# Retention's sample queries as a column of ones against weighted states

## The chip, the cores and the metric

The kernel runs on one core of a Trainium2 chip, as one launch. The metric is the device time of that launch in microseconds (us). A core has TensorE (PE, matrix products into PSUM; its weight loads are listed apart as PEld), VectorE (DVE), ScalarE (ACT), GpSimd (POOL) and SyncE (SP), which here issues the DMAs. Each engine runs its own queue of instructions in order, and semaphores tie the queues together.

## The reference

The reference is one layer of a decoder trunk: a half-step feed-forward block, a mixer, and a second half-step feed-forward block, each followed by a layer norm. The mixer adds a retention branch (8 heads of 256) and an HGRN2 branch (16 heads of 128). There are 272 prompt tokens (16 of them learned meta tokens) and 8 sample tokens; each sample has its own recurrent state, which is read, updated, written out and queried. For a sample, the chunk has one token, so retention comes down to this:

```python
def retention_chunk(S, q, k, v):
    C = q.shape[2]
    lg = retention_log_decay()
    ...
    o = jnp.einsum('bhij,bhjv->bhiv', inner, v) + jnp.einsum('bhid,bhdv->bhiv', q_dec, S)
    ...
    S_new = jnp.exp(lg * C)[:, None, None].astype(S.dtype) * S + jnp.einsum('bhjd,bhjv->bhdv', k_dec, v)
    return S_new.astype(S.dtype), o
```

With one token the two terms of `o` together are the query times the new state: o[v] = sum over d of q[d] * S_new[d, v], with d and v from 0 to 255. That sum, for 8 samples and 8 heads, is what the change computes in another way. It is followed by the head's layer norm (subtract the mean over v, divide by the deviation).

## The kernel before

All activations are kept with the features on the 128 partitions and the 280 tokens (272 and 8) along the free dimension. All large weights are streamed from memory in units of eight 128x128 blocks (512 KB): SyncE loads `raw` (line 185), ScalarE rounds it to `whi` (line 188), VectorE takes the rest `wlo` (line 189), and TensorE multiplies three times for each block, `whi` by the high and low part of the activations and `wlo` by the high part (line 218). `raw`, `whi` and `wlo` have three buffers each.

TensorE's order is the order of the program. The instructions of all other engines are ordered by the compiler's scheduler by readiness and priority; the weight stream has high priority. In the mixer the projections run group by group, and small steps of the two branches are put between their matmuls by hand: `mix_hg` and `mix_ret` are generators, one for each head pair or head `u`, and after each step k of a projection `pump` is called once. A `yield n` in a generator means that it goes on n pump calls later. A pump call comes after the blocks of one k, so after six matmuls where the group has two outputs.

`mix_ret(u, ...)` for head `u`: the states of the 8 samples come in four tiles `sms[2 * e + c]` of tag `smr`, where `e` is the half of the samples (0 to 3, 4 to 7) and `c` the chunk of 128 of the 256 state rows d. A tile has 128 partitions (d) by 4 samples by 256 columns (v). ScalarE multiplies each tile with the decay (line 1192), VectorE adds key times value (line 1198, one instruction for each sample and chunk), and SyncE writes the tile to the output `srs` (line 1202). The tag `smr` has four buffers, which `ks` and `vs`, two operands of the prompt's state, use as well.

After some more pump calls come the sample queries into the PSUM bank `pq` (tile name `pqr`): the score product of the last 16 prompt tokens (`scores`, line 1141), and then, for each sample and chunk, a matmul with a 128x32 stationary operand cut from `qdr`, in which one column holds the sample's query and the others are zero. The output goes to the 32 PSUM partitions `32 * j`, so that four samples can be in four column groups of the array at a time; each group adds up two samples (e = 0 and 1), in row e of its 32, and two chunks. These are 16 matmuls of 256 columns for each head, and each of these float32 matmuls stands in the trace as two records. The helper `alone` copies the queries into `qdr` before that. Then ScalarE copies the bank to `os` (line 1217), VectorE centres it, and seven pump calls later the head's output `por` is built.

Of the kernel before, what the change touches and what calls it, by code (L numbers as in the profile page):

```python
# [13 lines left out]
AF = mybir.ActivationFunctionType  # L14
ALU = mybir.AluOpType
# [3 lines left out]
P = 128  # L19
# [4 lines left out]
NMETA, SEQ, NS = 16, 256, 8  # L24
# [27 lines left out]
ALONE = 4 * 32 + 1  # L52
# [76 lines left out]
def trunk(ctx: ExitStack, tc: tile.TileContext, A, O):  # L129
    nc = tc.nc  # L130
# [12 lines left out]
    def mx_bank(name):  # L143
        return ps_m.tile([P, 512], F32, tag="mx", name=name)
# [94 lines left out]
    def mul(out, a, b):  # L239
        nc.vector.tensor_tensor(out=out, in0=a, in1=b, op=ALU.mult)  # L240
# [306 lines left out]
    with tc.tile_pool(name="yp", bufs=1) as yp:  # L547
# [7 lines left out]
        with tc.tile_pool(name="mp", bufs=1) as mp:  # L555
# [7 lines left out]
            def tmp(name, shape=(P, T), bufs=1, dt=F32, tag=None):  # L563
                if name in rows:
                    rows[name] = rows[name][1:] + rows[name][:1]
                    return rp.tile(list(shape), dt, tag=rows[name][-1], name=name)
                return mp.tile(list(shape), dt, tag=tag or name, name=name, bufs=bufs)
# [19 lines left out]


            qdh = tmp("qdh", (P, 4, ALONE))
            qdr = tmp("qdr", (P, 4, ALONE))  # L590
            nc.gpsimd.memset(qdh, 0.0)
            nc.gpsimd.memset(qdr, 0.0)
            qdh_at = [qdh.rearrange("p a c -> p (a c)")[:, 256 * h :] for h in range(2)]
            qdr_at = [qdr.rearrange("p a c -> p (a c)")[:, 2 * ALONE * c :] for c in range(2)]
            vsm = tmp("vsm", (P, P))
            vt2 = tmp("vt2", (P, 2, P))
            scr2 = tmp("scr2", (P, NMETA))
# [50 lines left out]
            def evacuate(n, c0, c1, o0, o1, b0, b1):  # L648
# [33 lines left out]
                elif n == "v_r":  # L682
                    v = tmp("v", (P, 2, T))
                    nc.scalar.copy(v[:, 0, :], o0)
                    nc.scalar.copy(v[:, 1, :], o1)
                    start(mix_ret(c0 // 2, st["q_r"], st["k_r"], v), 24 if c0 == 2 else 3)
                elif n in ("g_r", "g_h"):
                    sg = tmp("gs", (P, TL), bufs=2)
                    t = tmp("gt", (P, TL), bufs=2)
                    nc.scalar.activation(sg, o0, AF.Sigmoid)  # L690
                    mul(t, sg, o0)
                    sa = tmp("gs", (P, TL), bufs=2)
                    nc.scalar.activation(sa, o1, AF.Sigmoid)
                    mul(t, t, sa)
                    u, e = divmod(c0, 2)
                    while u not in (done_r if n == "g_r" else done_h):
                        pump()
                    if n == "g_r":
                        y = tmp("y", (P, TL))
                        mul(y, t, on_r[u][:, e, :])  # L700
                        st["y"] = y
                    else:
                        y = st["y"]
                        nc.vector.scalar_tensor_tensor(
                            out=t, in0=t, scalar=ngt[:, c0 : c0 + 1], in1=on_h[u][:, e, :], op0=ALU.mult, op1=ALU.mult)

                        ys[c0] = y if c0 < EARLY else yp.tile([P, TL], F32, tag=f"y{c0}", name=f"y{c0}")
                        add(ys[c0], y, t)
                        if c0 < EARLY:
                            split(yh[c0], yl[c0], y)  # L710
# [22 lines left out]
            def alone(qd, q):  # L733
                nc.vector.tensor_copy(
                    qd[:, :, : 128 : 32].rearrange("p (c e) j -> p c e j", e=2),
                    q[:, :, SEQ:].rearrange("p c (e j) -> p c e j", e=2))
# [348 lines left out]
            def mix_ret(u, q, k, v):  # L1085
# [3 lines left out]
                calm = 2  # L1089
                sms = []  # L1090
# [13 lines left out]
                for c in range(2):  # L1104
# [22 lines left out]
                    for x, g, his, i, lo in todo:  # L1127
                        for hi in his:
                            nc.scalar.activation(hi, x, AF.Copy, scale=g)
                        nc.vector.scalar_tensor_tensor(  # L1130
                            out=lo, in0=x, scalar=g, in1=his[i].bitcast(F32), op0=ALU.mult, op1=ALU.subtract)
                    yield 2
                alone(qdr, q)
                vts = [vt[:, 0], vt[:, 1], vs2]
                vrow = rows_out(vt2.rearrange("p c f -> p (c f)")[16:24, :], 256, "vr")

# [25 lines left out]
                for c in range(2):  # L1162
# [9 lines left out]
                    if c == 0:  # L1172
                        gams = [tmp("gam", (P, 1))]
                        nc.gpsimd.tensor_scalar(
                            out=gams[0], in0=so[:, 0:1], scalar1=GAMMA[u], scalar2=GAMMA[u], op0=ALU.min, op1=ALU.max)
# [13 lines left out]
                for e in range(2):  # L1189
# [3 lines left out]
                    for i in (2 * e, 2 * e + 1):  # L1193
                        for c in range(2):
                            for b in (2 * i, 2 * i + 1):
# [3 lines left out]
                                    out=x, in0=vbs[i][:, b - 2 * i, :], scalar=kk, in1=x, op0=ALU.mult, op1=ALU.add)  # L1199
# [1 line left out]
                    for c in range(2):  # L1201
                        nc.sync.dma_start(O["srs"][u, c, :, 4 * e : 4 * e + 4, :], ss[c])
                    yield 1 if e else 10 if u == 0 else 6
                yield (11 if u == 0 else 15) + 2 * calm
                pq = mx_bank("pqr")
                scores(pq[:, 256:], 2)
                for e in range(2):
                    for c in range(2):
                        for j in range(4):
                            b = 4 * e + j  # L1210
                            nc.tensor.matmul(  # L1211
                                pq[32 * j : 32 * j + 32, :256], qdr_at[c][:, 32 * b : 32 * b + 32],
                                sms[2 * e + c][:, j, :], start=e + c == 0, stop=e + c == 2, tile_position=(0, 32 * j))
                mul(scr2[:NB2], pq[:NB2, 256 : 256 + NMETA], dt[:NB2, c2:])
                upper_upper_lower(sc2, scr2[:NB2])
                os = tmp("osr", (P, 256))
# [160 lines left out]
```

## Time and profile before

| | |
|---|---|
| Time, median of 3 runs | 2567.76 us (2565.30 to 2568.72) |
| Profiled execution, span from its first to its last instruction | 2563.9 us |
| Granted TensorE clock | 1.000 |
| TensorE busy | 2553.4 us |
| VectorE busy | 1702.8 us |
| ScalarE busy | 1392.2 us |
| Sample-query matmuls `pqr<-smr,qdr` | 256 records, first at 859.8 us, last at 1698.6 us |

The profile is one execution. Its span leaves out what lies ahead of the first and behind the last instruction; the runs' times are 1.4 to 4.8 us above it. Rows of the timeline give the start in us, how long the row's instructions took together, the engine, the line, the operation with output and inputs by name, and how many instructions there are; in brackets stands the idle time ahead of it and what ended it. SPq marks the DMA issues of SyncE. Rows of groups give the count, then busy us and mean ns of one, then idle us before them. Rows of a tile give minimum, median and maximum ns.

### The profile page before, as it was taken

Reading aid. Unit: us, or ns where it says so; the run is one execution under the profiler, and the core shown is the slowest. Engines: PE = TensorE matmul, PEld = TensorE weight load, DVE = VectorE, ACT = ScalarE, POOL = GpSimd, SP = SyncE. Lnnn points to the kernel's source line nnn. Section 1 sums busy time; section 2 is a strip of 40 time slices with the busy share of each in tenths; the row PEclk is TensorE's granted clock in tenths of the full one; section 3 lists DMA queues with packets and bytes.
Section 4 is the critical chain, followed back from the end, with each engine's and each line's share of the span. In section 5 each row is a group of like instructions: output and inputs, shape, how many; then the busy total and the mean of one; then the engine's idle time right before and its main releaser. Section 6 shows DMA issues by size and latency. Waiting matters only on the chain.

```text
span 2563.9 us, 56275 instructions
## 1 busy us (share of the span) xinstructions
PE 2553.4 (100%) x23424; PEld 2534.4 (99%) x23424; DVE 1702.8 (66%) x2827; ACT 1392.2 (54%) x2186; POOL 57.0 (2%) x152
## 2 busy tenths in 40 slices
PE   9999999999999999999999999999999999999999
PEld 9999999999999999999999999999999999999998
DVE  6444544475569878777777777777885555556555
ACT  5444444444456767767676666675564444444443
POOL 0000000000000000000000000000000000000000
PEclk9999999999999999999999999999999999999999
DMA  7555555555555876767676767675556565565554
GB/s 244 183 187 183 187 182 184 186 182 186 184 201 180 287 265 232 264 214 260 212 264 215 259 223 255 224 239 188 196 190 197 194 197 195 194 196 195 195 195 149
DMA packets 156897, 536.26 MB, mean 209 GB/s; under 512 B 17952, under 2 KB 25952, under 8 KB 156640
## 3 DMA queue, kind: packets, MB, share of 16 engines
q1 hardware_dynamic: 156352, 532.37, 62.0%
q8 instruction: 183, 3.00, 0.5%
q14 instruction: 74, 0.61, 0.1%
q10 hardware_dynamic: 288, 0.29, 0.0%
HBM read 501.99 MB, written 30.61 MB: 208 GB/s over the span
## 4 chain that ended last, share of the span: by engine, by line
PE 96%; DVE 2%; ACT 0%; issue 0%; DMA 0%; SPq 0%; ACTq 0%; DVEq 0%
PE up L218 36%; PE dn L218 19%; PE pj_i_h L218 3%; PE pj_g_r L218 3%; PE pj_q_h L218 3%; PE pj_g_h L218 3%; PE pj_a_r L218 3%; PE pj_a_h L218 3%; PE pj_f L218 3%; PE pj_q_r L218 3%; PE pj_k_r L218 3%; PE wo L218 3%; PE pj_v_r L218 3%; DVE wlo L189 1%; PE pqr L1211 1%; PE psr L1168 0%
## 5 line engine op out<-in xcount | busy, mean ns | idle before, releaser
L189 DVE TENSOR_TENSOR wlo<-raw,whi 128x1024 fp32r<-128x1024 f32 (+1 forms) x869 | 1062.2, 1223 | 740.7 <-ACT whi L188 737.3
L188 ACT CAST whi<-raw 128x1024 fp32r<-128x1024 f32 (+1 forms) x870 | 905.7, 1042 | 909.2 <-PE up L218 411.0
L218 PE MATMUL up<-xh,whi 128*128 128x280 f32 (+1 forms) x2624 | 725.6, 280 | 0.6 <-ACT whi L188 0.6
L218 PE MATMUL up<-xh,wlo 128*128 128x280 f32 (+1 forms) x2624 | 725.8, 280 | 0.4 <-DVE wlo L189 0.3
L218 PE MATMUL up<-xl,whi 128*128 128x280 f32 (+1 forms) x2624 | 725.4, 279 | 0.0
L218 PEld LDWEIGHTS up<-xh,wlo 128*128 128x128 f32 x2624 | 492.6, 189 | 1.0 <-DVE wlo L189 1.0
L218 PEld LDWEIGHTS up<-xh,whi 128*128 128x128 f32 x2624 | 492.6, 189 | 0.8 <-ACT whi L188 0.8
L218 PEld LDWEIGHTS up<-xl,whi 128*128 128x128 f32 x2624 | 492.6, 189 | 0.0
L218 PE MATMUL dn<-hh,whi 128*128 128x280 f32 (+1 forms) x1376 | 384.7, 280 | 0.0
L218 PE MATMUL dn<-hh,wlo 128*128 128x280 f32 (+1 forms) x1376 | 384.3, 279 | 0.0
L218 PE MATMUL dn<-hl,whi 128*128 128x280 f32 (+1 forms) x1376 | 384.3, 279 | 0.0
L218 PEld LDWEIGHTS dn<-hh,whi 128*128 128x128 f32 x1376 | 260.1, 189 | 0.1
L218 PEld LDWEIGHTS dn<-hl,whi 128*128 128x128 f32 x1376 | 260.1, 189 | 0.1
L218 PEld LDWEIGHTS dn<-hh,wlo 128*128 128x128 f32 x1376 | 260.1, 189 | 0.0
L218 PE MATMUL pj_k_r<-xh,whi 128*128 128x280 f32 x256 | 74.2, 290 | 0.0
L218 PE MATMUL pj_g_r<-xh,whi 128*128 128x264 f32 x256 | 74.0, 289 | 0.0
L218 PE MATMUL pj_v_r<-xh,whi 128*128 128x280 f32 x256 | 73.8, 288 | 0.0
L218 PE MATMUL pj_v_r<-xh,wlo 128*128 128x280 f32 x256 | 72.4, 283 | 0.3 <-DVE wlo L189 0.3
L218 PE MATMUL pj_g_h<-xh,whi 128*128 128x264 f32 x256 | 72.7, 284 | 0.0
L218 PE MATMUL pj_k_r<-xh,wlo 128*128 128x280 f32 x256 | 72.4, 283 | 0.0
L218 PE MATMUL pj_v_r<-xl,whi 128*128 128x280 f32 x256 | 72.3, 283 | 0.0
L218 PE MATMUL pj_k_r<-xl,whi 128*128 128x280 f32 x256 | 72.3, 283 | 0.0
(421 smaller groups left out, 5263.4 us busy)
## 6 DMA issues: line engine op xcount, KB each, us to landing
raw<-in_w_up SPq DMA_DIRECT2D x343, 512.0 KB, 4.1
raw<-in_w_in SPq DMA_DIRECT2D x320, 512.0 KB, 4.3
raw<-in_w_dn SPq DMA_DIRECT2D x172, 512.0 KB, 3.5
smr<-in_sr SPq DMA_DIRECT2D x32, 512.0 KB, 5.0
out_srs<-smr SPq DMA_DIRECT2D x32, 512.0 KB, 6.7
raw<-in_w_out SPq DMA_DIRECT2D x32, 512.0 KB, 3.9
vbr<-vrd SPq DMA_DIRECT2D x32, 256.0 KB, 4.1
smh<-in_sg SPq DMA_DIRECT2D x16, 512.0 KB, 5.2
```

The source lines that it names most:

```text
L188: nc.scalar.copy(hi[:, j:jn, :], raw[:, j:jn, :])
L189: nc.vector.tensor_tensor(out=lo[:, j0:j1, :], in0=raw[:, j0:j1, :], in1=hi[:, j0:j1, :].bitcast(F32), op=ALU.subtract)
L218: nc.tensor.matmul(o, w, t, start=start, stop=stop)
L1211: nc.tensor.matmul(pq[32 * j : 32 * j + 32, :256], qdr_at[c][:, 32 * b : 32 * b + 32], sms[2 * e + c][:, j, :], start=e + c == 0, stop=e + ...
```

## The change

ScalarE multiplies the new state's chunk 0 in place with the sample's query (a scale for each partition), and VectorE adds chunk 1 times its part of the query, into the same tile. TensorE then needs only the sum over the 128 partitions: a stationary operand `one` with a column of ones in column e takes the place of `qdr`, and there are 8 matmuls for each head in place of 16. The weighting of e = 0 is placed 10 pump calls (head 0) or 14 (other heads) after the last state's update, that of e = 1 five later, and the matmuls five after that; before, the matmuls came after 15 or 19. `alone` is no longer called for retention.

```diff
             qdh = tmp("qdh", (P, 4, ALONE))
-            qdr = tmp("qdr", (P, 4, ALONE))
+            one = tmp("one", (P, 2, 32))
             nc.gpsimd.memset(qdh, 0.0)
-            nc.gpsimd.memset(qdr, 0.0)
+            nc.gpsimd.memset(one, 0.0)
+            for e in range(2):
+                nc.gpsimd.memset(one[:, e, e : e + 1], 1.0)
             qdh_at = [qdh.rearrange("p a c -> p (a c)")[:, 256 * h :] for h in range(2)]
-            qdr_at = [qdr.rearrange("p a c -> p (a c)")[:, 2 * ALONE * c :] for c in range(2)]
...
-                alone(qdr, q)
...
-                yield (11 if u == 0 else 15) + 2 * calm
+                yield (6 if u == 0 else 10) + 2 * calm
+                for e in range(2):
+                    s0, s1 = sms[2 * e : 2 * e + 2]
+                    for b in range(4):
+                        g = [q[:, c, SEQ + 4 * e + b : SEQ + 4 * e + b + 1] for c in range(2)]
+                        nc.scalar.activation(s0[:, b, :], s0[:, b, :], AF.Copy, scale=g[0])
+                        nc.vector.scalar_tensor_tensor(
+                            out=s0[:, b, :], in0=s1[:, b, :], scalar=g[1], in1=s0[:, b, :], op0=ALU.mult, op1=ALU.add)
+                    yield 5
                 pq = mx_bank("pqr")
                 scores(pq[:, 256:], 2)
                 for e in range(2):
-                    for c in range(2):
-                        for j in range(4):
-                            b = 4 * e + j
-                            nc.tensor.matmul(
-                                pq[32 * j : 32 * j + 32, :256], qdr_at[c][:, 32 * b : 32 * b + 32],
-                                sms[2 * e + c][:, j, :], start=e + c == 0, stop=e + c == 2, tile_position=(0, 32 * j))
+                    for j in range(4):
+                        nc.tensor.matmul(
+                            pq[32 * j : 32 * j + 32, :256], one[:, e, :], sms[2 * e][:, j, :],
+                            start=e == 0, stop=e == 1, tile_position=(0, 32 * j))
```

## The prediction

> **What bounds the kernel now.** I read the page first (busy times and the chain that ended last), then who waits for whom on TensorE, then the work of this step in order of time on TensorE, SyncE, VectorE and ScalarE.
>
> ```profile
> span 2563.9 us, 56275 instructions
> PE 2553.4 (100%) x23424; PEld 2534.4 (99%) x23424; DVE 1702.8 (66%) x2827; ACT 1392.2 (54%) x2186; POOL 57.0 (2%) x152
> ...
> PE 96%; DVE 2%; ACT 0%; issue 0%; DMA 0%; SPq 0%; ACTq 0%; DVEq 0%
> ```
>
> TensorE is busy in 2553.4 of 2563.9 us, and the chain is TensorE for 96%. So a matmul less is time less, as long as nothing makes TensorE wait. Its waits on other engines begin with these rows:
>
> ```profile
> PE pw L515 <- DVE eps_h L163: 1.0, 1, 1.0
> PE pt L1116 <- POOL tails L1103: 0.9, 1, 0.9
> PE pj_f L218 <- DVE wlo L189: 0.7, 1, 0.7
> ```
>
> No wait is longer than 1.0 us: any new wait of some microseconds per head would be a new thing in this profile. The mixer, where the change lies, is tighter than the whole:
>
> ```profile
> 820.00:1750.00 930.00, 929.82 (x9489) 915.63 (x9490) 737.92 (x1483) 634.12 (x1198) 50.37 (x119) 1.00 0.71 242
> 1180.00:1190.00 10.00, 10.00 (x92) 10.00 (x91) 8.28 (x15) 5.09 (x7) 0.00 (x0) 1.00 0.91 296
> ```
>
> The columns are length, busy PE, PEld, DVE, ACT and POOL, granted clock, DMA share, GB/s. VectorE is busy 738 of 930 us (79%), and in the ten microseconds ahead of a head's sample queries (second row, head 3) the DMA engines are 91% busy.
>
> **The change, part by part.**
>
> *TensorE does half of the sample-query matmuls.* Head 3 stands for all eight; five of its rows:
>
> ```profile
> 1190.65 1.08 PE L1039 MATMUL pq<-smh,qdh 128*32 128x128 f32 x32
> 1191.55 0.23 PE L1141 MATMUL pqr<-q_r,k_r 128*16 128x16 f32 x3
> 1191.60 0.42 PE L1211 MATMUL pqr<-smr,qdr 128*32 128x256 f32 x3
> ...
> 1193.69 0.28 PE L218 MATMUL pj_g_r<-xl,whi 128*128 128x264 f32 x1
> 1193.80 0.28 PE L218 MATMUL pj_g_r<-xh,wlo 128*128 128x264 f32 x1
> ```
>
> Sixteen matmuls are 32 records, and they hold TensorE from 1191.60 until the projection goes on at about 1193.5, some 1.9 us. Sixteen records of the same 256 columns remain. That is as many columns as the 32 records of 128 that HGRN2's queries take in the row above, and those hold TensorE for 0.90 us (1190.65 to 1191.55). So a head saves between 0.8 us (half of 32 records less the ends) and 1.0; I take 0.83, and 8 x 0.83 = 6.6 us for the kernel.
>
> *ScalarE and VectorE get 64 instructions each.* No row has these exact instructions; the nearest:
>
> ```profile
> L998 ACT ACTIVATE smh<-smh,meta 128x128 f32<-128x128 f32 x128 | 41.1, 391 | 0.4
> L1192 ACT ACTIVATE smr<-smr,sro 128x1024 f32<-128x1024 f32 x16 | 18.2, 1147 | 7.5 <-DMA smr<-in_sr 7.4
> L1198 DVE SCALAR_TENSOR_TENSOR smr<-vbr,sro,smr 128x256 f32<-128x256 f32 x64 | 27.5, 478 | 1.9 <-DMA vbr<-vrd 1.8
> ...
> L734 DVE COPY qdr<-q_r x8: 174/175/178, 812.3 to 1644.4; 128x16 f32<-128x16 f32 x8
> ```
>
> An activation of 256 columns with a scale from memory lies between 0.39 us (128 columns) and 1.15 (1024); on the line between them it is 0.50. The scalar_tensor_tensor is the L1198 shape, 0.48. So ScalarE gets 64 x 0.50 = 32 us and VectorE 64 x 0.48 = 31 us, less 8 x 0.175 = 1.4 us of copies into `qdr`. VectorE goes from 79% to about 82% of the mixer and ScalarE from 68% to about 72%: as a sum this is hidden behind TensorE's 930 us. If the cover were gone at these places, it would cost up to 4 us a head. The memset of `qdr` on GpSimd goes, two small ones come, all in GpSimd's idle time: nothing.
>
> *The queries move five pump calls later* (10+5+5 in place of 15, and 14+5+5 in place of 19, with the 4 of `2 * calm` in each). A pump comes after six matmuls of 0.11 us (the two projection rows above), so five are 30 x 0.1126 = 3.4 us. Everything after the queries moves with them: score product, `os`, `por`, the norm. The last head has 80 pumps until its gates need the result; its steps take 62 and will take 67. Nothing is late. On SyncE the next head's two loads into the states' buffers wait for these matmuls (row 1194.19 below) and go later with them; they are used some 100 us later.
>
> *A new wait: ScalarE now overwrites states that are still on their way out.* This decides the case. `s0` is in place: the weighting writes the tile that the out-DMA `srs` reads, so it must wait until that DMA has landed. Today nothing waits for that landing but the buffer's next user. Head 3, SyncE's queue, and the DMA's time to landing over all heads:
>
> ```profile
> 1185.84 3.00 SPq L185 DMA_DIRECT2D raw<-in_w_in  x2
> 1188.89 0.43 SPq L1202 DMA_DIRECT2D out_srs<-smr  x1
> 1191.35 0.33 SPq L185 DMA_DIRECT2D raw<-in_w_in  x1
> 1191.73 0.49 SPq L1202 DMA_DIRECT2D out_srs<-smr  x1
> 1193.81 0.33 SPq L185 DMA_DIRECT2D raw<-in_w_in  x1
> 1194.19 1.27 SPq L1095 DMA_DIRECT2D smr<-in_sr  x2
> ...
> DMA to landing us min/median/max: 6.4/6.7/7.3
> ```
>
> ```profile
> 1184.59 1.22 DVE L189 TENSOR_TENSOR wlo<-raw,whi 128x1024 fp32r<-128x1024 f32 x1
> 1185.73 1.27 DVE L1198 SCALAR_TENSOR_TENSOR smr<-vbr,sro,smr 128x256 f32<-128x256 f32 x3
> 1187.26 1.22 DVE L189 TENSOR_TENSOR wlo<-raw,whi 128x1024 fp32r<-128x1024 f32 x1
> ```
>
> The row at 1188.89 is the DMA of `s0` of samples 4 to 7 (e = 1). Its states were ready after the first of the three instructions at 1185.73, so at about 1186.2; it then stood on SyncE behind a weight load until 1188.89. It lands at 1188.89 + 6.7 = 1195.6. Then ScalarE weights four states (0.50 + 3 x 0.40; neighbours overlap), VectorE's last addition takes 0.48: ready at 1195.6 + 2.2 = 1197.8, and the last matmul adds 0.2: 1198.0. Unhindered, the moved queries would start at 1191.55 + 3.4 = 1194.95 and take 0.9, to 1195.85. TensorE is in order, so it stands for 2.15 us. The other heads, by the same sum, from their own two rows (out-DMA of e = 1, first matmul of the queries):
>
> ```profile
> 854.47 0.80 SPq L1202 DMA_DIRECT2D out_srs<-smr  x1
> 945.28 0.34 SPq L1202 DMA_DIRECT2D out_srs<-smr  x1
> 1061.85 0.43 SPq L1202 DMA_DIRECT2D out_srs<-smr  x1
> 1694.38 0.42 SPq L1202 DMA_DIRECT2D out_srs<-smr  x1
> ```
>
> ```profile
> 859.70 0.24 PE L1141 MATMUL pqr<-q_r,k_r 128*16 128x16 f32 x3
> 950.15 0.21 PE L1141 MATMUL pqr<-q_r,k_r 128*16 128x16 f32 x2
> 1065.21 0.23 PE L1141 MATMUL pqr<-q_r,k_r 128*16 128x16 f32 x3
> 1696.95 0.23 PE L1141 MATMUL pqr<-q_r,k_r 128*16 128x16 f32 x3
> ```
>
> Ready plus last matmul is issue + 9.1; the unhindered end is first matmul + 4.3. Head 0: 863.6 against 864.0, no stall; head 1: 954.4 against 954.4, none; head 2: 1.4; head 7: 2.2; heads 3 to 6 lie between 1.8 and 2.2. Six heads make 11.8 us.
>
> That sum gives ScalarE and VectorE to the chain alone. They also split the weights, and where such an instruction falls between, the chain grows by 1.0 or 1.2 us. The upper end is 11.8 + 6 x 2.2 = 25 us, the lower end 0 (the first rival). VectorE splits a unit every 2.7 us (1184.59, 1187.26), and the chain is 2.2 us long, so about half the heads should meet one: I take 15 us.
>
> **Sum:** -6.6 (TensorE) + 15 (stalls) + 0 (VectorE and ScalarE elsewhere) = +8.4 us. On the profiled execution's span that is 2563.9 to 2572.3; the median of the runs shown, 2567.8, is 3.9 us above that span, which gives 2576 us.
>
> **The rivals.**
>
> *Faster: the wait is hidden anyway.* If the out-DMA of e = 1 left at 1186.2, when its states are ready, rather than behind the weight load, it would land at 1192.9 and be weighted by 1195.1, before an unhindered end at 1195.85. No stall remains: 2567.8 - 6.6 = 2561. For it: the order on SyncE is made anew for the changed program, and 2.7 us there decide it. Against it: the weight load stands in front of this DMA in all six late heads, and nothing in the change comes before it in the program. Chance 0.2. The Trainium skill ("Perfetto Trace Analysis", Identifying Performance Opportunities) holds that a kernel improves with its most-contended engine, here TensorE; by that rule this is the outcome. The Trainium skill ("DMA: Bandwidth & Descriptors", Anatomy of one DMA) prices a DMA issued by GpSimd at 2.0 us plus its bytes at 436 GB/s, an estimate of 3.2 us for these 512 KB; by it no head would stall, but the measured 6.7 us decides.
>
> *No difference.* The stalls come to between 1.5 and 11.7 us (some heads covered, no weight split in between), and eat the saving. Chance 0.2; 2568.
>
> *Much slower: the wait hits the weight stream too.* ScalarE waits in order. The weighting of e = 0 comes where the casts of the weights come, and these are already late:
>
> ```profile
> 1185.35 1.05 ACT L188 CAST whi<-raw 128x1024 fp32r<-128x1024 f32 x1 [1.97 <-DMA raw<-in_w_in]
> 1189.02 1.05 ACT L188 CAST whi<-raw 128x1024 fp32r<-128x1024 f32 x1 [2.33 <-DMA raw<-in_w_in]
> ...
> 1180.31 0.42 SPq L1202 DMA_DIRECT2D out_srs<-smr  x1
> ```
>
> The out-DMA of e = 0 lands at 1180.31 + 6.7 = 1187.0. If the weighting is queued ahead of the cast at 1185.35, that cast, the `wlo` behind it and TensorE are up to 1.6 + 1.6 = 3.2 us late, say 2.2 in each of six heads: 13 us more, 2589. It decides if more than three of the six heads have that order. Against it: in the next gap, 1186.7 to 1189.0, ScalarE idles and the weighting fits. Chance 0.2.
>
> **How the numbers follow.** The likeliest case has 0.4 and gives 2576, by itself 2571 to 2585. The range 2560 to 2592 takes in both ends. Changes under 0.2% (5.1 us) cannot be told from none here. Slower is 0.4 + 0.2 = 0.6, the same 0.2, faster 0.2.
>
> **What would show it.** Right: `pqr` has 128 records in place of 256; TensorE shows a wait of 1 to 4 us for the states (VectorE's new line) in heads 2 to 7 and little in 0 and 1; ScalarE's new line waits for the `srs` DMA. Wrong: if TensorE never waits for the states, I mis-set the out-DMA's time or its order on SyncE; if TensorE waits for `wlo` in the mixer instead, it is the third rival.

## The result and the profile after

The changed kernel takes 2587.78 us (median of 4 runs, 2585.46 to 2589.25) against 2567.28 us (4 runs, 2565.30 to 2568.72). The ratio is 1.008, with a 95% interval of 1.0066 to 1.0095: slower by 20.5 us. The profiled execution is the shortest of the four (2585.46 us, span 2583.7).

The page of the changed kernel, in the parts shown of before:

```profile
span 2583.7 us, 56151 instructions
PE 2558.8 (99%) x23296; PEld 2534.8 (98%) x23296; DVE 1725.7 (67%) x2883; ACT 1415.5 (55%) x2250; POOL 59.4 (2%) x154
...
PE 57%; DVE 3%; DMA 3%; issue 2%; ACT 2%; POOL 0%; SPq 0%; ACTq 0%; DVEq 0%; POOLq 0%
```

TensorE has 128 matmul records less, and yet 5.4 us more busy time than before; 24.9 us of its span are idle, 10.5 before. A matmul that runs slowly counts as busy, so the busy time does not show the whole loss. A DMA has 3% of the chain that ended last, 0% before, and the page's split by line names it: out_srs<-smr, 2%. Who waited for whom, TensorE's longest waits first, and then the new one of ScalarE (columns: total us, times, longest us):

```profile
PE por L1232 <- DVE sc L255: 5.2, 1, 5.2
PE pj_g_r L218 <- DVE wlo L189: 3.7, 5, 1.0
PE pj_g_h L218 <- DVE wlo L189: 3.0, 5, 0.8
...
ACT smr L1209 <- DMA out_srs<-smr: 48.7, 16, 5.5
```

Line 1209 is the weighting: ScalarE stood 48.7 us for the out-DMAs, in all eight heads and for both halves of the samples. TensorE's own wait for the weighted states is short: 2.2 us, in eight waits of its weight loads (the rows below, of the queries' tile). Idle time understates this wait, since matmul records overlap. From the first record of a head's queries (its score product) to the projection's next matmul it takes 1.07 us in every head of half_only (below), where nothing is waited for; in the changed kernel it is 2.3, 2.4 and 1.8 us in heads 2, 5 and 6 and 1.1 to 1.2 in the others, 3.4 us more in all. The rest of TensorE's waits are for `wlo`, the weights' low part, and for `por` in head 0.

```profile
L1217 PE MATMUL pqr<-smr,one x128: 379/379/404, 863.2 to 1721.7; 128*32 128x256 f32 x128
...
  DVE smr L1210: 2.2, 8
```

Head 3 in the changed kernel, ScalarE and then SyncE:

```profile
1192.77 1.05 ACT L188 CAST whi<-raw 128x1024 fp32r<-128x1024 f32 x1 [0.18 <-PE pj_a_h L218]
1199.04 0.51 ACT L1209 ACTIVATE smr<-smr,q_r 128x256 f32<-128x256 f32 x1 [5.22 <-DMA out_srs<-smr]
1199.45 0.37 ACT L691 ACTIVATE gs<-pj_g_h 128x264 f32<-128x264 f32 x1
1199.72 1.03 ACT L188 CAST whi<-raw 128x1024 fp32r<-128x1024 f32 x1
...
1204.22 0.51 ACT L1209 ACTIVATE smr<-smr,q_r 128x256 f32<-128x256 f32 x1 [1.05 <-DMA out_srs<-smr]
```

```profile
1192.46 0.42 SPq L1202 DMA_DIRECT2D out_srs<-smr  x1
...
1194.26 1.18 SPq L1202 DMA_DIRECT2D out_srs<-smr  x1
1196.99 0.33 SPq L185 DMA_DIRECT2D raw<-in_w_in  x1
1197.38 0.48 SPq L1202 DMA_DIRECT2D out_srs<-smr  x1
1202.04 3.00 SPq L185 DMA_DIRECT2D raw<-in_w_in  x2
```

The out-DMA of e = 0 is issued at 1192.46, and ScalarE goes on at 1199.04, 6.6 us later. Behind the waiting instruction stand a gate's `gs` and the cast at 1199.72, which comes almost 7 us after the cast before it; a unit of weights lasts TensorE about 2.7 us. The out-DMA of e = 1 now leaves at 1197.38, ahead of the two weight loads at 1202.04: the order on SyncE, which the prediction's sum rested on, is another. In heads 3 to 7 the first out-DMA of e = 1 now follows the last of e = 0 after 3.1 to 3.9 us with one weight load between them; before it was 5.8 to 6.4 us, with two.

Where the time came from is worked out for each head: the projection's matmuls (line 218) are the same 20832 in all kernels, and the start of one of them after a head's queries and output, less its start in the kernel before, is what has been lost up to there. The two columns on the right are these differences in us, from one profiled execution each, which can be up to 3 us off the median (that of wait_only is its slowest run, that of own_best its fastest). Times are medians; each ratio is against runs of the kernel before on the same chip, whose medians were 2566.8 to 2567.8.

| kernel | time, us | ratio to before (interval) | head 0 | heads 1 to 7 |
|---|---|---|---|---|
| changed | 2587.8 | 1.008 (1.0066 to 1.0095) | +8.7 | +11.5 |
| moved_only | 2577.4 | 1.0043 (1.0030 to 1.0056) | +8.7 | +3.2 |
| wait_only | 2584.5 | 1.0067 (1.0053 to 1.0081) | +10.3 | +10.0 |
| half_only | 2562.8 | 0.9983 (0.9974 to 0.9991) | -0.9 | -1.8 |
| own_tile | 2572.4 | 1.0020 (1.0011 to 1.0029) | +2.4 | +2.1 |
| own_e0 | 2580.3 | 1.0051 (1.0037 to 1.0065) | +8.4 | +6.3 |
| por_later | 2578.0 | 1.0046 (1.0034 to 1.0059) | +4.1 | +9.9 |
| gpsimd_first | 2599.6 | 1.0128 (1.0114 to 1.0142) | +13.3 | +20.6 |
| own_early | 2564.8 | 0.9992 (0.9983 to 1.0001) | -0.9 | -1.1 |
| own_best | 2564.3 | 0.9988 (0.9979 to 0.9997) | -0.9 | -2.9 |

### The profile page after: what moved, and what is told of

Read it like the earlier page. It is cut to its first block, busy times and chain, and to the rows that moved or that the text cites. A ratio compares the mean times of both kernels' runs of the same rounds, so it can differ in the third digit from the quotient of the medians.

```text
span 2583.7 us, 56151 instructions
## 1 busy us (share of the span) xinstructions
PE 2558.8 (99%) x23296; PEld 2534.8 (98%) x23296; DVE 1725.7 (67%) x2883; ACT 1415.5 (55%) x2250; POOL 59.4 (2%) x154
## 4 chain that ended last, share of the span: by engine, by line
PE 57%; DVE 3%; DMA 3%; issue 2%; ACT 2%; POOL 0%; SPq 0%; ACTq 0%; DVEq 0%; POOLq 0%
PE up L218 17%; PE dn L218 9%; PE pj_k_r L218 3%; PE wo L218 3%; PE pj_v_r L218 3%; PE pj_g_r L218 2%; PE pj_q_r L218 2%; PE pj_a_r L218 2%; PE pj_f L218 2%; PE pj_g_h L218 2%; PE pj_a_h L218 2%; PE pj_q_h L218 2%; PE pj_i_h L218 2%; DMA out_srs<-smr 2%; DVE wlo L189 1%
## 5 line engine op out<-in xcount | busy, mean ns | idle before, releaser
L218 PE MATMUL pj_g_r<-xh,wlo 128*128 128x264 f32 x256 | 71.4, 279 | 3.8 <-DVE wlo L189 3.7
L218 PE MATMUL pj_g_h<-xh,wlo 128*128 128x264 f32 x256 | 71.2, 278 | 3.0 <-DVE wlo L189 3.0
```

The source lines that it names most:

```text
L218: nc.tensor.matmul(o, w, t, start=start, stop=stop)
```

## The experiments

**moved_only: the kernel before, five pump calls later.**

```diff
-                yield (11 if u == 0 else 15) + 2 * calm
+                yield (16 if u == 0 else 20) + 2 * calm
```

> The kernel before with its 16 matmuls and no weighting, only five pump calls later. Theory (in head 0 the late queries' score product and output fall among the HGRN2 sample updates of the same engines, whatever the weighting does): 8 us in head 0, nothing elsewhere, 2575 us (2572 to 2577). Rival (head 0's loss needs the weighting's wait as well): 2567 to 2569 us.

It takes 2577.4 us, 10 us more than before and just above the expected range, since the other heads lose 3.2 us too. Head 0 alone loses 8.7 us, as much as in the changed kernel. VectorE in head 0, first in the kernel before, then in moved_only, and TensorE in moved_only:

```profile
862.12 0.15 DVE L240 TENSOR_TENSOR scr<-pqr,dtab 16x16 f32<-16x16 f32 x1
862.54 0.17 DVE L255 TENSOR_TENSOR sc<-scr,sc 16x16 fp32r<-16x16 f32 x1 [0.27 <-ACT sc L723]
...
867.90 0.88 DVE L999 SCALAR_TENSOR_TENSOR smh<-vbh,meta,smh 128x128 f32<-128x128 f32 x3
```

```profile
868.63 1.40 DVE L999 SCALAR_TENSOR_TENSOR smh<-vbh,meta,smh 128x128 f32<-128x128 f32 x5
870.07 0.16 DVE L240 TENSOR_TENSOR scr<-pqr,dtab 16x16 f32<-16x16 f32 x1
872.92 0.61 DVE L999 SCALAR_TENSOR_TENSOR smh<-vbh,meta,smh 128x128 f32<-128x128 f32 x2 [2.69 <-ACT smh L998]
873.56 0.17 DVE L255 TENSOR_TENSOR sc<-scr,sc 16x16 fp32r<-16x16 f32 x1
...
876.34 0.42 DVE L1083 TENSOR_TENSOR osr<-osr,cen 128x256 f32<-128x256 f32 x1
```

```profile
863.01 1.89 PE L1211 MATMUL pqr<-smr,qdr 128*32 128x256 f32 x29
...
869.66 0.84 PE L1226 MATMUL por<-dtab,vtr 128*128 128x256 f32 x4
873.88 0.25 PE L1226 MATMUL por<-sc,vs 128*128 128x16 f32 x1 [3.37 <-DVE sc L255]
876.90 0.45 PE L741 MATMUL por<-ident,osr 128*128 128x128 f32 x1 [2.78 <-DVE osr L1083]
```

Before, `scr` and `sc` were done by 862.7, five microseconds ahead of HGRN2's sample updates (`smh`). Five pump calls later they queue behind the `smh` work, on ScalarE as on VectorE. `por` follows seven pump calls after the queries and stands for `sc` and for the centred `osr`, 6.2 us together. These 6.2 us are not all of the 8.7. Here are two matmuls of the projection after the stop, and a stretch around them (length, busy PE, granted clock, DMA share, GB/s):

```profile
877.36 0.43 PE L218 MATMUL pj_q_r<-xl,whi 128*128 128x264 f32 x1
877.58 0.43 PE L218 MATMUL pj_q_r<-xh,wlo 128*128 128x264 f32 x1
```

```profile
874.50:881.30 6.80, 4.40 (x19) 0.50 0.62 223
```

The granted clock is 0.50 from 874.5 to 881.3 us, and the matmuls start 0.22 us apart in place of 0.11. TensorE has work again from 877.0 on, so about half of the 4.3 us up to 881.3 is lost, an estimate of 2.2 us; with the 6.2 that makes 8.4 of the 8.7. The changed kernel and own_e0 have the same 6.8 us at this clock in head 0, wait_only 10.2. In own_tile and por_later, where TensorE waits for `por` 2.9 us and less, the clock stays at 1.00 there. No run varies the stop alone, so what makes the clock fall is not shown.

The loss of head 0 needs no weighting. How large it is depends on the order of the other engines' instructions as well: own_tile has the queries at the same place and loses 2.4 us. Head 1 loses 1.2 us in moved_only, and heads 2 to 7 lose 0.3 to 0.4 each: there the queries stood directly behind HGRN2's queries (`pq`), and at a place of their own they break the projection a second time.

**por_later: the changed kernel, with head 0's output later.**

```diff
-                yield 7
+                yield 7 if u else 15
```

> The changed kernel, in head 0 alone with 15 in place of 7 pump calls between the sample queries and the head's output por; all else as in the change. Theory (head 0 loses because por needs sc and the centred os, which stand on VectorE and ScalarE behind HGRN2's sample updates): TensorE's waits of por (5.2 us for sc, 1.0 for osr) go, 2579 to 2583 us. Rival (the engines are that much behind, and another instruction of TensorE waits instead): 2586 to 2589 us.

2578.0 us, 9.8 less than the changed kernel and a little more gain than expected. No wait of `por` is among TensorE's longest now, and head 0 loses 4.1 in place of 8.7 us. The profiles show 5.7 us between the two kernels (2578.0 and 2583.7), the medians 9.8; the profiled execution of the changed kernel was its shortest. In head 0 the granted clock stays at 1.00; of what it still loses, 1.9 us is a wait of `pq` for `Sh`. Head 6 loses 4.1 us in this profile, 2.4 of them at the queries: from their first record to the projection's next matmul it takes 3.5 us in place of 1.07, because the weighted states are late.

**wait_only: the wait without the work.** The old matmuls at the new place, and two tiny instructions a head in place of the weighting:

```diff
-                yield (11 if u == 0 else 15) + 2 * calm
+                yield (6 if u == 0 else 10) + 2 * calm
+                for e in range(2):
+                    nc.scalar.activation(sms[2 * e][:, :, :1], sms[2 * e][:, :, :1], AF.Copy, scale=1.0)
+                    yield 5
```

> The kernel before with its 16 matmuls a head, the queries five pump calls later as in the change, and in place of the weighting only two ScalarE instructions a head (4 elements a partition, times one, in place on the s0 tiles), which must wait for the out-DMA as the weighting does. No additions on VectorE. Theory: the wait alone holds up the casts, so ScalarE waits some 40 to 50 us for srs in all and the time is 2582 to 2592 us (2567.3 + 8 for head 0 + some 7 to 17 for the other heads). Rival (the added work, not the wait): like the kernel with the move alone, 2567 to 2576 us.

```profile
PE pj_g_r L218 <- DVE wlo L189: 3.6, 6, 0.8
...
ACT smr L1206 <- DMA out_srs<-smr: 68.2, 16, 5.8
```

2584.5 us, 7.1 more than moved_only, which has everything but the wait. Sixteen instructions on four elements a partition bring the `wlo` waits back. Heads 1 to 7 lose 10.0 us in place of moved_only's 3.2, so an instruction on ScalarE that waits for the landing is enough to cost them 6.8 us. It is not shown to be all: in the changed kernel heads 1 to 7 lose 11.5 us although TensorE saves 7 x 0.86 = 6.0 there, which is 14.3 us beyond the move's 3.2.

**own_tile: the work without the wait.** The weighted states go into free buffers (`wt`: three of tag `vbr`, which gets a third buffer, and two rotary rows):

```diff
...
-                        nc.scalar.activation(s0[:, b, :], s0[:, b, :], AF.Copy, scale=g[0])
+                        nc.scalar.activation(wt, s0[:, b, :], AF.Copy, scale=g[0])
                         nc.vector.scalar_tensor_tensor(
-                            out=s0[:, b, :], in0=s1[:, b, :], scalar=g[1], in1=s0[:, b, :], op0=ALU.mult, op1=ALU.add)
+                            out=wt, in0=s1[:, b, :], scalar=g[1], in1=wt, op0=ALU.mult, op1=ALU.add)
...
-                            pq[32 * j : 32 * j + 32, :256], one[:, e, :], sms[2 * e][:, j, :],
+                            pq[32 * j : 32 * j + 32, :256], one[:, e, :], ws[4 * e + j],
```

> The changed kernel, but ScalarE writes the weighted states into free buffers (three of the value rows, the two rotary rows) and VectorE adds there, so that nothing overwrites a state that its out-DMA still reads. The 64 activations, 64 additions and the 8 matmuls a head stay. Theory (ScalarE stands in order behind the out-DMA's landing and holds up the weight casts): the 48.7 us of ScalarE waiting for srs go, heads 1 to 7 lose nothing and keep their saving, head 0 still pays its late output; 2587.8 - 17 = about 2570 us (2565 to 2574). Rival (the 64 + 64 added instructions themselves overload VectorE and ScalarE where the weights have no lead): no change, 2584 to 2590 us.

2572.4 us, 15.4 less than the changed kernel with the same instructions. No engine's wait for out_srs is left among the long ones. The rival that the added work overloads the engines falls as the main cause. The time is in the expected range, but not by the expected parts. Of the 15.4 us, 6.3 are in head 0, which was to keep its loss. Heads 1 to 7 lose 9.4 us less, but were to gain: 6.0 us saved less 3.2 for the move is 2.8, and they lose 2.1, so some 4.9 us stay with the added work at this place. TensorE still waits there for `wlo` (2.2 us in `pj_g_h`).

**own_e0: which landing it is.** Free buffers for e = 0 alone:

```diff
...
+                        if e:
+                            ws.append(s0[:, b, :])
+                        else:
+                            if b % 2 == 0:
+                                wv = tmp("vbr", (P, 2, 256), bufs=2)
+                            ws.append(wv[:, b % 2, :])
...
```

> The changed kernel with free buffers for the weighted states of e = 0 alone (two value rows); e = 1 is weighted in place and waits for its out-DMA as in the change. The step in the prediction's sum (the landing for e = 1 stops TensorE at the queries): most of the loss of heads 1 to 7 stays, 2580 to 2588 us. The prediction's third rival (the landing for e = 0 stops ScalarE while the weight casts have no lead): it goes, 2570 to 2576 us.

2580.3 us, at the edge of the first expectation, and neither is right as it stood. Heads 1 to 7 lose 6.3 us in place of 11.5 (own_tile: 2.1): of the 9.4 us that both landings cost, 5.2 go with e = 0 and 4.2 with e = 1. The landing for e = 1 acts where the prediction put it, at the queries, though for less time. ScalarE waits for it, and then TensorE's weight loads wait for the states:

```profile
PE pqr L1225 <- DVE smr L1218: 0.5, 2, 0.3
...
PEld pqr L1225 <- DVE smr L1218: 3.8, 11, 0.8
...
ACT smr L1217 <- DMA out_srs<-smr: 23.9, 8, 4.3
```

Head 2 in half_only, then in own_e0:

```profile
1064.64 0.23 PE L1141 MATMUL pqr<-q_r,k_r 128*16 128x16 f32 x3
...
1065.70 0.38 PE L218 MATMUL pj_g_r<-xh,whi 128*128 128x264 f32 x1
```

```profile
1079.19 0.24 PE L1141 MATMUL pqr<-q_r,k_r 128*16 128x16 f32 x3
...
1080.18 1.82 PE L1225 MATMUL pqr<-smr,one 128*32 128x256 f32 x8 [0.28 <-DVE smr L1218]
1081.93 0.38 PE L218 MATMUL pj_g_h<-xh,whi 128*128 128x264 f32 x1
```

The queries hold TensorE for 2.74 us in place of 1.06, though PE is idle for only 0.28 of them. Over the eight heads it is 5.0 us more than in half_only, 3.3 of them in heads 2 and 6. The landing for e = 0 acts on the projection. Added up over heads 1 to 7, the distances between neighbouring matmuls of the projection with nothing else of TensorE's between them have grown by 12.9 us in the changed kernel, by 5.9 in own_e0 and by 6.2 in own_tile: without the wait for e = 0 this loss is no larger than in own_tile, which has neither wait.

**gpsimd_first: the wait in another queue.** The first weighting, in place, on GpSimd:

```diff
-                        nc.scalar.activation(s0[:, b, :], s0[:, b, :], AF.Copy, scale=g[0])
+                        nc.gpsimd.tensor_scalar(
+                            out=s0[:, b, :], in0=s0[:, b, :], scalar1=g[0], scalar2=None, op0=ALU.mult)
```

> The changed kernel with the first weighting (state times query, in place) on GpSimd in place of ScalarE, so that the wait for the out-DMA's landing stands in the queue of an engine that has little else. VectorE's addition stays. If the wait costs because it stands in ScalarE's queue before the casts: near own_tile, 2570 to 2576 us. If VectorE, which waits for GpSimd in order and has wlo behind it, takes the wait up: 2580 to 2590 us.

```profile
L1209 POOL TENSOR_SCALAR smr<-smr,q_r x64: 917/925/2147, 850.9 to 1734.2; 128x256 f32<-128x256 f32 x64
```

```profile
PE pj_g_r L218 <- DVE wlo L189: 7.6, 6, 2.5
...
POOL smr L1209 <- DMA out_srs<-smr: 85.7, 10, 15.1
...
DVE smr L1211 <- POOL smr L1209: 18.9, 32, 3.2
```

2599.6 us, worse than both expectations. The wait has only changed queues: VectorE's additions wait for GpSimd, 32 times, and `wlo` stands behind them. GpSimd also takes 0.92 us for an instruction that takes ScalarE 0.50, so part of the loss is its slowness. And the granted clock is 0.50 in three stretches of this profile, 17.0 us in all. The wait, the slowness and the clock were not separated.

**half_only: TensorE's saving alone.** No weighting (the product with the query is left out), and the 8 matmuls at the old place.

```diff
-                yield (6 if u == 0 else 10) + 2 * calm
+                yield (1 if u == 0 else 5) + 2 * calm
...
-                        nc.scalar.activation(s0[:, b, :], s0[:, b, :], AF.Copy, scale=g[0])
-                        nc.vector.scalar_tensor_tensor(
-                            out=s0[:, b, :], in0=s1[:, b, :], scalar=g[1], in1=s0[:, b, :], op0=ALU.mult, op1=ALU.add)
+                        pass
```

> The changed kernel without any weighting (the sample queries' result is left out: the matmuls sum the chunk-0 states unweighted), the 8 matmuls at the place where the kernel before has its 16. Theory: TensorE's saving alone, 8 x 0.83 = 6.6 us: 2560.7 us (2559 to 2562). Rival (the saving is hidden or smaller, since the first matmuls and the switch set the length): 2564 to 2567 us.

2562.8 us, 4.6 less than before: between the two expectations. At each of the eight places TensorE gains 0.86 us, 6.9 in all. The profiled execution gives 4.2 of it back, 1.7 in each of heads 5 and 6, where the projection waits for a weight. TensorE's longest wait, and ScalarE ahead of it in head 5:

```profile
PE pj_g_h L218 <- DVE wlo L189: 1.5, 2, 0.8
```

```profile
1428.44 1.15 ACT L1192 ACTIVATE smr<-smr,sro 128x1024 f32<-128x1024 f32 x1 [2.79 <-DMA smr<-in_sr]
1429.50 1.03 ACT L188 CAST whi<-raw 128x1024 fp32r<-128x1024 f32 x1
```

ScalarE stands 2.8 us for a load of states in each of these two heads (0.4 in the kernel before), and the cast stands behind it. TensorE is 3.1 and 2.2 us earlier there than before; the load lands 0.6 us earlier and 0.2 later. So this loss, too, is a wait for a DMA in ScalarE's queue ahead of a cast.

**own_early and own_best: the version without either loss.** own_tile with the queries where they were, the weighting ahead of them; in own_best head 1's queries are three pump calls later, because TensorE stood there for the states.

```diff
-                yield (6 if u == 0 else 10) + 2 * calm
+                yield (1 if u == 0 else 5) + 2 * calm
```

```diff
-                yield (1 if u == 0 else 5) + 2 * calm
+                yield (1, 8)[u] + 2 * calm if u < 2 else 5 + 2 * calm
```

> The changed kernel with the weighted states in free buffers (as in own_tile), and the queries back at the pump calls where the kernel before has them (the weighting 10 and 5 calls ahead of them). Theory: with no landing to wait for, the weighting is done in time, head 0 loses nothing (its score product is again ahead of the HGRN2 sample updates), and the queries follow HGRN2's own again, which saves the 0.3 us a head that a separate place costs; TensorE's saving of 0.86 a head is left, less some waits for wlo: 2562 to 2566 us. Rival (the weighting costs the weight stream as much as TensorE saves, wherever it stands): 2569 to 2573 us, like own_tile.

> own_early with the queries of head 1 alone three pump calls later (8 in place of 5), since there TensorE still stood about 1.5 us for the states. Theory (what is left of the loss is that one wait): head 1 goes from +2.2 to about 0, 2563.5 us, ratio to before 0.998 to 0.999. Rival (the weight stream takes it back in that stretch, where its loads are late): as own_early, 2565 us.

own_early takes 2564.8 us, which cannot be told from before (0.9983 to 1.0001), and 7.6 us less than own_tile. own_best takes 2564.3 us, against 2567.8 of the runs of before beside it: 0.9988 (0.9979 to 0.9997), faster than the kernel before by a margin that is barely clear. own_early is 2.0 us above half_only, which has no weighting, but the intervals of the two ratios overlap. Between own_early and own_best, head 1 goes from +2.1 to +0.8 us, less than expected; the medians do not separate them. TensorE's longest waits in own_best:

```profile
PE pj_g_h L218 <- DVE wlo L189: 1.2, 3, 0.5
PE pw L515 <- DVE eps_h L163: 1.0, 1, 1.0
```

## Why the prediction was right in sign and under half in size

The forecast was 2576 us and slower; 2587.8 is inside the range and 11.8 us above the number. Point by point:

- *TensorE saves 0.83 us a head.* Right: 0.86 in half_only. But the sum took the whole of it as gain, and moved_only shows that a place of its own costs 0.3 us a head again, and half_only that late casts take some of it back.
- *64 instructions on each engine, hidden.* Right in their price. They measured 0.50 and 0.48 us:

```profile
L1209 ACT ACTIVATE smr<-smr,q_r x64: 492/502/512, 850.1 to 1718.5; 128x256 f32<-128x256 f32 x64
L1210 DVE SCALAR_TENSOR_TENSOR smr<-smr,q_r x64: 474/478/485, 854.5 to 1719.9; 128x256 f32<-128x256 f32 x64
```

  At the old place they are hidden: own_early, which has all of them, is not slower than before. At the place of the change some 4.9 us of own_tile's loss stay with them.
- *Everything after the queries moves, nothing is late.* Wrong, and the largest term that was left out. The step counted pump calls up to the head's gates and did not ask what stands on VectorE and ScalarE at the new place. In head 0 that is HGRN2's sample updates, and the move alone costs 8.7 us, about a quarter of it by the granted clock. With 3.2 us in the other heads it is 11.9, booked at nothing. That this is about the size of the whole miss is chance, since the other terms were off too.
- *A new wait for the out-DMA's landing.* Right as a cause: 16 waits, 48.7 us on ScalarE. Right only in part in the place and the size. The sum let TensorE stand for the states at the queries, 11.8 us in six heads and 15 with the weights' splits; it stood there 3.4 us longer than in half_only, in heads 2, 5 and 6 for the most part, and not the 1 to 4 us in each of heads 2 to 7. The step that failed is the one that kept the order on SyncE: in heads 3 to 7 the out-DMA of e = 1 left one weight load earlier, as in the first rival. And the wait for e = 0 held the casts, as in the third. That rival was priced at 2.2 us in six heads; taking this wait out (own_e0) is worth 5.2 us in seven. Heads 1 to 7 lost 11.5 us net of a saving of 7 x 0.86 = 6.0, so 17.5 gross: 3.2 for the move, 9.4 for the two landings, and 4.9 for the added work at this place. The rival's total, 2589 us, is near the measured one, but partly by chance: it held 15 us of stalls at the queries where 3.4 came, and lacked the 8.7 of head 0.
- *The landing itself.* 6.7 us was taken; in the changed kernel it was less:

```profile
DMA to landing us min/median/max: 5.1/6.1/6.5
```

  The Trainium skill ("DMA: Bandwidth & Descriptors", Anatomy of one DMA) says that the semaphore cannot fire before the last byte has landed at its target. No run here separates that from the reading of the source, which is all that ScalarE needed: it was released 6.6 us after the issue in head 3. The price that the Trainium skill gives in the same section for a DMA that GpSimd issues, an estimate of 3.2 us for these bytes, was not met by these, which SyncE issues: they took 6.1 us.
- *The rule for the other side.* The Trainium skill ("Perfetto Trace Analysis", Identifying Performance Opportunities) says that improving a kernel generally means improving its most-contended engine. Here TensorE's work was cut, and the kernel got slower; with the waits for the landing and the move both taken out (own_best), the cut is worth 3.5 us of the 6.9 that TensorE saves.

Shown by experiment: that the move is enough to cost head 0 its 8.7 us (moved_only), that the wait without the work costs the other heads 6.8 us (wait_only), and that taking the two waits out gives them back 9.4 (own_tile), about half for each (own_e0). That `wlo` is the link between ScalarE's wait for e = 0 and TensorE is read from the waits, in the changed kernel and in wait_only. Open are the 4.9 us that stay with the added work, and what makes the clock fall in head 0.

## What to carry to other kernels

Before writing in place into a buffer that an output DMA reads, look at which engine's queue will hold the wait for the landing, and at what stands behind it: a tile of its own, even from borrowed buffers, made the same work nearly free here (own_early). When a step is moved, look at the queues of all engines that its followers use at the new place, not only at whether its result is needed later. After a stop of the main engine, look at its granted clock too, and read a wait for small matmuls from the time to the next instruction, not from idle time alone. On a kernel whose main engine is busy 99.6% of the time, a saving of 0.3% can be smaller than the cost of where the step is put.

## What was not expected of the hardware

- Around the end of two stops of 3.4 and 2.8 us in head 0, the granted clock of TensorE was 0.50 for 6.8 us, and its matmuls then started 0.22 us apart in place of 0.11 (moved_only): 6.2 us of waiting became a loss of 8.7.
- GpSimd took 0.92 us (median) for a 128x256 float32 multiplication by a scale for each partition, with up to 2.15 us; ScalarE took 0.50 for the same.
- A short group of float32 matmuls put at a place of its own in the projection costs 0.3 to 0.4 us more than one put directly behind another such group (moved_only, heads 2 to 7).
